# Row sums of a 64 MiB tensor: splitting the rows 112 and 16 per partition instead of 120 and 8

## The chip, the cores and the metric

The kernel runs on one core of one Trainium2 chip. The metric is device time in microseconds (us), span of the program plus what the launch adds; lower is better.

## The reference

```python
batch, seq, dim = 32, 512, 1024
x = np.random.randn(batch, seq, dim).astype(np.float32)     # 16384 rows of 4 KiB, 67.1 MB
divisor = float(dim)

def reference(x, divisor):
    return (np.sum(x, axis=-1) / divisor).astype(np.float32)   # 16384 numbers
```

Every byte of `x` has to come from HBM once, and almost nothing goes back (64 KiB).

## The kernel before

Each of the 128 partitions gets 128 rows. They are cut in two parts: a main part of `M` = 120 rows per partition, contiguous in HBM for each partition, and a last part of `L` = 8 rows per partition. The main part's sums are stored while the last part is still on its way; the sums of the last part leave in a small store at the very end. Pieces get smaller towards the end, so that little work is left when the last bytes arrive. VectorE sums most rows; ScalarE takes some of the late ones (`on_act`), through an activation that also accumulates.

```python
    L = 8
    M = J - L                                      # J = 128
    x_main = bass.AP(tensor=x.tensor, offset=0, ap=[[M * D, P], [D, M], [1, D]])
    x_last = bass.AP(tensor=x.tensor, offset=P * M * D, ap=[[L * D, P], [D, L], [1, D]])
    o_main = bass.AP(tensor=out.tensor, offset=0, ap=[[M, P], [1, M]])
    o_last = bass.AP(tensor=out.tensor, offset=P * M, ap=[[L, P], [1, L]])

    main = [(2, 0)] + [(14, 0)] * 6 + [(14, 4), (12, 5), (8, 4)]     # (rows, of them on ScalarE)
    last = [(4, 2), (2, 1)]
    bulk = ctx.enter_context(tc.tile_pool(name="bulk", bufs=3))
    one = ctx.enter_context(tc.tile_pool(name="one", bufs=1))
    # ... PSUM pool for the activations' unused output
    res = one.tile([P, M], F32, name="res")        # sums of the main part
    fin = one.tile([P, L], F32, name="fin")        # finished sums of the last part
    q = one.tile([P, L], F32, name="q")
    r = one.tile([P, L], F32, name="r")
    nc.gpsimd.memset(r, 0.0)

    j = 0
    for rows, on_act in main:
        t = bulk.tile([P, 14, D], F32, name="t")
        load(t[:, :rows, :], x_main[:, j : j + rows, :])
        sums(res[:, j : j + rows], t, rows, on_act)
        j += rows
    j = 0
    for rows, on_act in last:
        t = one.tile([P, rows, D], F32, name=f"t{rows}")
        load(t, x_last[:, j : j + rows, :])
        sums(q[:, j : j + rows], t, rows, on_act)
        j += rows
    # ... then one whole row (tile row), and the last row in three parts (pa, pb, pc), all loaded from x_last
    nc.gpsimd.tensor_scalar_mul(out=res, in0=res, scalar1=scale)
    tc.keep_in_program_order(nc.sync.dma_start(out=o_main, in_=res))      # the large store
    # ... sums of the last row's parts; fin = q * scale + r; the last column of fin
    tc.keep_in_program_order(nc.sync.dma_start(out=o_last, in_=fin))      # the last store
```

## Time and profile before

| | before |
|---|---|
| median of runs | 161.48 us (three runs, 161.44 to 161.75; with a fourth run: 161.50) |
| span in the profile | 159.9 us |
| VectorE busy | 121.1 us (76%) |
| ScalarE busy | 19.7 us (12%) |
| read from HBM | 67.11 MB, 420 GB/s over the span |

How to read it: no compute engine is busy throughout (VectorE, the busiest, has 76% of the span), and the DMA row of the page is at 9 tenths or more in 32 of the 40 slices. The lines themselves are in the prediction below.

Two more things can be taken from the trace that no view prints. It has a record of each DMA packet (one run of bytes of one partition, with its start and duration; a 14-row load is 128 packets of 57344 B, eight on each of the 16 DMA engines), and the time at which each of the 16 engines reports its share of a load as landed.

### The profile page before, as it was taken

The page shows a single profiled execution, that of the slowest core. Times are in us where ns is not written, and L with a number is a line of the kernel's source. Part 1 is how long each engine was busy: PE and PEld are TensorE (multiplying, and loading weights), DVE is VectorE, ACT ScalarE, POOL GpSimd, SP SyncE. Part 2 cuts the span into 40 slices and gives each one's busy share as a digit, 9 for nine tenths or more (in the row PEclk, how much of TensorE's full clock was granted, in tenths as well). Part 3 has the DMA queues.
Part 4 walks back from the last instruction along what each step waited for, and adds up shares of the span by engine and source line. Part 5 has one row for each costly group of instructions (what it writes and reads, how often), then busy time and mean ns, then how long its engine had stood idle before and what let it go on. Part 6 is the DMA issues. An engine that isn't in the chain of part 4 may idle for free.

```text
span 159.9 us, 139 instructions
## 1 busy us (share of the span) xinstructions
DVE 121.1 (76%) x17; ACT 19.7 (12%) x37; POOL 0.8 (1%) x6
## 2 busy tenths in 40 slices
DVE  0500059995999599968999699959995995494985
ACT  3000000000000000000000000000001900480973
POOL 0000000000000000000000000000000000000010
DMA  7999999987999999987999999987999999999993
GB/s 271 451 459 459 459 459 459 459 373 330 445 459 459 459 459 459 459 387 316 445 459 459 459 459 459 459 387 330 430 459 426 393 578 406 393 393 393 418 408 109
DMA packets 2592, 67.18 MB, mean 420 GB/s; under 512 B 544, under 2 KB 928, under 8 KB 1056
## 3 DMA queue, kind: packets, MB, share of 16 engines
q1 hardware_dynamic: 2592, 67.18, 97.9%
HBM read 67.11 MB, written 0.07 MB: 420 GB/s over the span
## 4 chain that ended last, share of the span: by engine, by line
DMA 77%; DVE 22%; SPq 1%; issue 0%; DVEq 0%
DMA t<-in_x_dram 56%; DMA row<-in_x_dram 21%; DVE res L153 20%; SPq L142 1%; DVE q L173 1%; DVE scaled L195 0%; DVE pc L190 0%; DVE fin L191 0%; DVEq L195 0%; DVEq L229 0%
## 5 line engine op out<-in xcount | busy, mean ns | idle before, releaser
L153 DVE TENSOR_REDUCE res<-t 128x14 f32<-128x14336 f32 (+4 forms) x10 | 115.7, 11566 | 36.4 <-DMA t<-in_x_dram 36.4
L147 ACT ACTIVATE junk<-t 128x1024 f32<-128x1024 f32 x16 | 16.2, 1014 | 136.0 <-DMA t<-in_x_dram 136.0
L153 DVE TENSOR_REDUCE q<-t 128x2 f32<-128x2048 f32 (+1 forms) x2 | 3.5, 1753 | 0.7 <-DMA t<-in_x_dram 0.7
L147 ACT ACTIVATION_READ_ACCUMULATOR junk<-t 128x1 f32 x16 | 3.0, 189 | 0.0
L147 ACT ACT_TABLE_LOAD x1 | 1.3, 1283 | 1.7 <-PEq L215 1.7
L186 POOL TENSOR_SCALAR res<-res 128x120 f32<-128x120 f32 x1 | 0.5, 513 | 150.3 <-DVE res L153 150.3
L173 DVE TENSOR_REDUCE q<-row 128x1 f32<-128x768 f32 x1 | 1.0, 953 | 0.1
L195 DVE TENSOR_SCALAR_CACHE_REDUCE scaled<-pc 128x322 f32<-128x322 f32 x1 | 0.5, 490 | 0.1
L147 ACT ACTIVATE junk<-pa 128x448 f32<-128x448 f32 x1 | 0.5, 548 | 0.1
L190 DVE TENSOR_REDUCE pc<-pb 128x1 f32<-128x256 f32 x1 | 0.4, 411 | 0.0
L147 ACT ACTIVATE junk<-row 128x256 f32<-128x256 f32 x1 | 0.4, 388 | 0.1
L191 DVE SCALAR_TENSOR_TENSOR fin<-q,r 128x7 f32<-128x7 f32 x1 | 0.2, 166 | 0.0
L147 ACT ACTIVATION_READ_ACCUMULATOR junk<-row 128x1 f32 x1 | 0.2, 187 | 0.0
L147 ACT ACTIVATION_READ_ACCUMULATOR junk<-pa 128x1 f32 x1 | 0.2, 187 | 0.0
L139 POOL MEMSET r<- 128x8 f32 x1 | 0.1, 105 | 1.3 <-POOLq L215 1.3
L215 POOL MEMSET const-bfloat16-1.0<- 128x1 bf16 x1 | 0.1, 103 | 0.0
L215 POOL MEMSET const-uint8-127<- 128x1 uint8 x1 | 0.1, 102 | 0.0
L215 POOL MEMSET const-float32-0.0<- 128x1 f32 x1 | 0.1, 99 | 0.2 <-issue 0.2
L215 POOL MEMSET const-float32-1.0<- 128x1 f32 x1 | 0.1, 99 | 0.0
L195 DVE DVE_READ_ACCUMULATOR scaled<-pc 128x1 f32 x1 | 0.1, 83 | 0.0
## 6 DMA issues: line engine op xcount, KB each, us to landing
t<-in_x_dram SPq DMA_DIRECT2D x7, 7168.0 KB, 35.7
t<-in_x_dram SPq DMA_DIRECT2D x1, 6144.0 KB, 33.3
t<-in_x_dram SPq DMA_DIRECT2D x1, 4096.0 KB, 26.0
t<-in_x_dram SPq DMA_DIRECT2D x2, 1024.0 KB, 18.7
t<-in_x_dram SPq DMA_DIRECT2D x1, 2048.0 KB, 30.6
row<-in_x_dram SPq DMA_DIRECT2D x1, 512.0 KB, 33.4
pa<-in_x_dram SPq DMA_DIRECT2D x1, 224.0 KB, 33.5
pc<-in_x_dram SPq DMA_DIRECT2D x1, 160.0 KB, 33.2
```

The costliest lines, as they stand in the source:

```text
L139: nc.gpsimd.memset(r, 0.0)
L142: tc.keep_in_program_order(nc.sync.dma_start(out=dst, in_=src))
L147: nc.scalar.activation(junk[:, :n], src, COPY, scale=by, accum_out=dst)
L153: nc.vector.reduce_sum(out=dst[:, :d], in_=t[:, :d, :], axis=AX)
L173: nc.vector.reduce_sum(out=q[:, j : j + 1], in_=row[:, :c], axis=AX)
L186: nc.gpsimd.tensor_scalar_mul(out=res, in0=res, scalar1=scale)
L190: nc.vector.reduce_sum(out=pc[:, D - b + 1 :], in_=pb, axis=AX)
L191: nc.vector.scalar_tensor_tensor(out=fin[:, : L - 1], in0=q[:, : L - 1], scalar=scale, in1=r[:, : L - 1], op0=MULT, op1=ADD)
L195: nc.vector.tensor_scalar(out=scaled, in0=pc, scalar1=scale, scalar2=0.0, op0=MULT, op1=ADD, accum_out=fin[:, L - 1 :])
L215: nc = _bacc.Bacc("TRN2", target_bir_lowering=False, num_devices=1)
```

## The change

The 8-row piece moves from the main part to the last part: 112 + 16 rows. Intent: the main result is complete one piece earlier, so that the large store is issued earlier; and the last store writes 64 B per partition instead of 32.

```diff
-    L = 8
+    L = 16
     M = J - L
@@
-    main = [(2, 0)] + [(14, 0)] * 6 + [(14, 4), (12, 5), (8, 4)]
-    last = [(4, 2), (2, 1)]
+    main = [(2, 0)] + [(14, 0)] * 6 + [(14, 4), (12, 5)]
+    last = [(8, 4), (4, 2), (2, 1)]
@@
     for rows, on_act in last:
-        t = one.tile([P, rows, D], F32, name=f"t{rows}")
+        if rows == 8:
+            t = bulk.tile([P, 14, D], F32, name="t")[:, :8, :]
+        else:
+            t = one.tile([P, rows, D], F32, name=f"t{rows}")
         load(t, x_last[:, j : j + rows, :])
```

## The prediction

> **What bounds the kernel now.** I read the page first (busy shares, DMA row, chain), then the timeline of the last third, then the chain in order of time, then the DMA issues. The page's chain:
>
> ```profile
> DVE 121.1 (76%) x17; ACT 19.7 (12%) x37; POOL 0.8 (1%) x6
> DMA packets 2592, 67.18 MB, mean 420 GB/s; under 512 B 544, under 2 KB 928, under 8 KB 1056
> DMA 77%; DVE 22%; SPq 1%; issue 0%; DVEq 0%
> ```
>
> No compute engine is full; DMA has 77% of the chain. That DVE has 22% is only how the chain is followed: it passes through reduces because a later load waits for a buffer. The timeline tells whether DVE truly delays the loads:
>
> ```profile
> 55.65 15.09 DVE L153 TENSOR_REDUCE res<-t 128x14 f32<-128x14336 f32 x1 [1.86 <-DMA t<-in_x_dram]
> 72.59 15.09 DVE L153 TENSOR_REDUCE res<-t 128x14 f32<-128x14336 f32 x1 [1.86 <-DMA t<-in_x_dram]
> 89.53 15.09 DVE L153 TENSOR_REDUCE res<-t 128x14 f32<-128x14336 f32 x1 [1.85 <-DMA t<-in_x_dram]
> ...
> 137.94 7.62 DVE L153 TENSOR_REDUCE res<-t 128x7 f32<-128x7168 f32 x1 [3.72 <-DMA t<-in_x_dram]
> ...
> 147.66 4.42 DVE L153 TENSOR_REDUCE res<-t 128x4 f32<-128x4096 f32 x1 [2.09 <-DMA t<-in_x_dram]
> ```
>
> It does not. Each 14-row reduce starts 16.94 us after the one before and lasts 15.09 us; the 1.85 us between is waiting for data. A 14-row load is 7.34 MB (7168 KB on the page), so the stream delivers 7.34 MB / 16.94 us = 433 GB/s. The later pieces come equally fast: the 8-row piece lands 147.66 - 137.94 = 9.72 us after the 12-row one, 4.19 MB / 9.72 us = 432 GB/s. So the load stream is one unbroken transfer, and only the start before it and the tail after it could change. The tail, from the chain in order of time:
>
> ```profile
> 122.95 33.36 DMA row<-in_x_dram
> 156.31 0.02 issue
> 156.34 0.96 DVE q L173
> 157.30 0.02 issue
> 157.32 0.17 DVE fin L191
> 157.49 0.34 DVE pc L190
> 157.83 0.04 DVEq L195
> 157.86 0.07 issue
> 157.93 0.49 DVE scaled L195
> 158.42 0.01 DVEq L229
> ```
>
> From the arrival of the last whole row (156.31) VectorE works serially until 158.42; the last store is issued at 158.46 and the span ends at 159.9. The two stores:
>
> ```profile
> out_dram<-res SPq DMA_DIRECT2D x1, 60.0 KB, 5.2
> out_dram<-fin SPq DMA_DIRECT2D x1, 4.0 KB, 1.4
> ```
>
> The 60 KB store is issued at 152.70 (timeline) and lands 5.2 us later, about 157.9. The 4 KB store takes 1.4 us from issue to landing and ends the span. Before issuing it, the sync engine waits for the landing of everything else, the 60 KB store included: that wait is met 0.55 us before VectorE's result is (158.44), so the 60 KB store is close to the end, but not on the path.
>
> [...]
> - [...]
> - [...] The stores' elements go from 480 to 448 B and from 32 to 64 B[...] (mean 8.5 ns for 32 B, 26.9 ns for 480 B in its packet records)[...].
> - [...] the 60 KB store, issued at 152.70, lands 0.2 us after the last load (issued 124.45, 33.2 us to landing, 157.65). It waited its turn behind loads issued 28 us earlier.
> - [...] Here the pitch goes from 480 to 448 KiB in the main part and from 32 to 64 KiB in the last part[...]. The trace before shows no pitch effect: the packet records of 57344 B (480 KiB pitch, 2118 ns) and 4096 B (32 KiB pitch, 161.9 ns) give (2118 - 161.9) / 53248 B = 0.03674 ns per byte and 11.4 ns fixed; that predicts 613 ns for the 16384 B packets of the 4-row load (32 KiB pitch, measured 614) and 1215 for the 32768 B ones (480 KiB pitch, measured 1215). One line fits both pitches.
>
> **The change part by part.** The order of instructions on each engine is the same, by count and kind, with the same waits; sizes and targets differ.
> 1. **Loads.** The same fifteen-odd transfers of the same sizes in the same order; only HBM addresses differ. By the line above a packet's time depends on its size alone: 0.
> 2. **The 8-row piece** (4-row reduce 4.42 us on VectorE, 4 rows x (1.01 + 0.19 overlapping) us on ScalarE) writes to the small tile instead of the main result. Same durations, same place: 0.
> 3. **The main result is complete one piece earlier.** GpSimd's scaling (0.51 us) waits for the reduce that now ends at 137.94 + 7.62 = 145.56 rather than 152.1; the store is issued near 146.1 + 0.05 rather than 152.70. But all loads have been issued by 124.9, so it still stands behind them in each ring, and lands right after the last one: about 157.87 instead of 157.88, its 8 packets per engine being 32 B smaller (32 x (26.9 - 8.5) / 448 = 1.3 ns each, 0.01 us in all). It has 0.55 us of slack, so 6.5 us of earlier issue buys 0 at the end.
> 4. **The combining operation on VectorE** (fin<-q,r) goes from 7 to 15 elements. VectorE's slope is (15086 - 2287) ns / 12288 elements = 1.04 ns per element, so +8 ns, on the serial tail.
> 5. **The last store** goes from 32 to 64 B per partition, 8 packets per engine. In the packet records it is issued at 158.46, its packets run from 159.30 to 159.49, and it lands at 159.87: 0.84 us to start, 0.19 us moving, 0.38 us confirming. Only the middle part depends on size: +1.3 ns x 8 = +0.01 us.
> 6. GpSimd's first fill, 16 instead of 8 columns, at 1.75 us: hidden, 0.
>
> Sum: 0.008 + 0.01 = +0.02 us, so 161.48 + 0.02 = **161.5 us**.
>
> **The rivals.**
> - **Wider elements make the last store quicker.** [...] 64 B ones might save part of the 0.38 us. I would not give it more than 0.2: 161.3 us. For it: this seems the intent. Against: 1.4 us is mostly fixed[...].
> - **The earlier store gets between the loads.** If the rings let it pass, its 8 packets x 26 ns = 0.2 us per engine come ahead of the last row, which shifts the tail: 161.7 us. Against: the 5.2 us wait in the ring seen before.
> - **The new pitch slows the last 16 rows.** They take 157.65 - 137.94 = 19.7 us. [...] Against: one line for two pitches, one of them the power of two 32 KiB[...]. For: this pitch is untried here.
> - **The 60 KB store was the true gate of the end.** Then freeing it would gain up to 0.5 us: 161.0 us. Against: it lands at 157.9, VectorE ends at 158.4, and it stays behind the loads anyway.
>
> **Range and chances.** The three runs before spread 161.44 to 161.75, 0.31 us, more than any effect that I sum. I add the two small rivals on either side (-0.2 and +0.2) to the scatter: 161.1 to 161.9 us. [...]
>
> **What would show each step.** In the changed profile: 14-row reduces still 16.94 us apart (step 1); the 8-row piece still landing about 9.7 us after the 12-row one and the last row at 156.3 (pitch; later means that rival); GpSimd's scaling near 145.6 and the store's time to landing grown from 5.2 to about 11.7 us (step 3; about 2 us to landing instead means that it passed the loads); the combining operation near 174 ns (step 4); the last store still at 1.4 us (step 5; 1.2 or less speaks for wide elements). The prediction is wrong if the last row's landing moves by more than 0.3 us or the last store by more than 0.2 us.

## The result, and the profile after

| | runs | median | all runs (us) |
|---|---|---|---|
| before | 4 | 161.50 | 161.48, 161.75, 161.44, 161.52 |
| after | 4 | 161.31 | 161.31, 161.27, 161.31, 161.58 |

The ratio is 0.9989, with a 95% interval of 0.9971 to 1.0006: the same within 2%, inside the predicted range of 161.1 to 161.9, and 0.19 us below the predicted 161.5. A ratio is the mean time of one kernel's runs over that of the other's of the same rounds, so not quite the ratio of the medians.

Now the lines after that answer to those of before. First the bulk and the pieces behind it, from the timeline of VectorE, with GpSimd's scaling (columns: start, duration, engine and line, operation, what it writes and reads; in brackets the idle time before it and what ended that):

```profile
106.47 15.09 DVE L153 TENSOR_REDUCE res<-t 128x14 f32<-128x14336 f32 x1 [1.85 <-DMA t<-in_x_dram]
...
145.65 0.49 POOL L189 TENSOR_SCALAR res<-res 128x112 f32<-128x112 f32 x1 [143.80 <-DVE res L153]
...
147.66 4.42 DVE L153 TENSOR_REDUCE q<-t 128x4 f32<-128x4096 f32 x1 [2.09 <-DMA t<-in_x_dram]
```

The 8-row piece is reduced at 147.66 exactly as before, and into `q` now; GpSimd scales at 145.65 instead of 152.16. Then the tail, from the chain in order of time:

```profile
122.91 33.25 DMA row<-in_x_dram
156.16 0.02 issue
156.18 0.96 DVE q L176
157.14 0.03 issue
157.17 0.18 DVE fin L194
157.34 0.34 DVE pc L193
157.68 0.04 DVEq L198
157.72 0.07 issue
157.79 0.49 DVE scaled L198
```

The tail is the same work, but it starts when the last whole row lands, at 156.16 instead of 156.31. From there to the last store's issue it takes 2.15 us in both (158.31 - 156.16; 158.46 - 156.31). Last, the two stores in the DMA view (size, and time from issue to landing):

```profile
out_dram<-res SPq DMA_DIRECT2D x1, 56.0 KB, 11.5
out_dram<-fin SPq DMA_DIRECT2D x1, 8.0 KB, 1.4
```

The large store waits 11.5 us instead of 5.2, and the wide last store takes 1.4 us as the narrow one did (1.42 against 1.41 in the trace). So neither of the intended effects reaches the end. Yet the last six loads took less time: from the landing of the 8-row piece (147.63 in both) to that of the last load 9.87 us instead of 10.04. I had expected nothing there, and the question for the experiments was whether that is real, and what makes it.

### The profile page after: what moved, and what is told of

It is laid out like the page before. It is cut to its first block, busy times and chain, and to the rows that moved or that the text cites. A ratio compares the mean times of both kernels' runs of the same rounds, so it can differ in the third digit from the quotient of the medians.

```text
span 159.8 us, 139 instructions
## 1 busy us (share of the span) xinstructions
DVE 121.1 (76%) x17; ACT 19.6 (12%) x37; POOL 0.8 (0%) x6
## 4 chain that ended last, share of the span: by engine, by line
DMA 76%; DVE 22%; SPq 1%; issue 0%; DVEq 0%
DMA t<-in_x_dram 56%; DMA row<-in_x_dram 21%; DVE res L153 20%; SPq L142 1%; DVE q L176 1%; DVE scaled L198 0%; DVE pc L193 0%; DVE fin L194 0%; DVEq L198 0%; DVEq L232 0%
## 5 line engine op out<-in xcount | busy, mean ns | idle before, releaser
L153 DVE TENSOR_REDUCE res<-t 128x14 f32<-128x14336 f32 (+3 forms) x9 | 111.2, 12360 | 34.3 <-DMA t<-in_x_dram 34.3
L153 DVE TENSOR_REDUCE q<-t 128x4 f32<-128x4096 f32 (+2 forms) x3 | 7.9, 2642 | 2.7 <-DMA t<-in_x_dram 2.5
L189 POOL TENSOR_SCALAR res<-res 128x112 f32<-128x112 f32 x1 | 0.5, 494 | 143.8 <-DVE res L153 143.8
```

Of the source, the lines that this page charges most:

```text
L153: nc.vector.reduce_sum(out=dst[:, :d], in_=t[:, :d, :], axis=AX)
```

## The experiments

The first four compare three theories. NOISE: nothing but scatter. ADDRESS: the new HBM addresses make the last loads quicker. STORE: the earlier store does. The first eleven runs were made on one chip; the kernel before had 161.38 us there in nine runs (161.26 to 161.45).

**1. The changed kernel once more.** No edit.

> The changed kernel once more, to learn whether its 0.19 us are real. Three theories. NOISE: the two kernels differ by nothing but scatter; ratio within 0.9990 to 1.0010, and in the trace the last whole row lands anywhere between 156.15 and 156.35. ADDRESS: the last loads read HBM at a pitch of 64 instead of 32 KiB and arrive a little sooner; ratio about 0.9988, and from the landing of the 8-row piece (147.63) to that of the last load about 9.87 us instead of 10.04. STORE: the large store, issued at 152.7 in the kernel before, disturbs the last loads, and issued at 146.2 it does so no more; same ratio of 0.9988. The prediction's rival that the wide last store gains is already at odds with the trace (1.42 against 1.41 us).

Measured: 161.34 us (161.26 to 161.37), ratio 0.9998 (0.9984 to 1.0011). The kernels are equal on this chip. But the last six loads were again quicker: 9.83 us. So the stage is not noise, although the whole time is hardly different: something else must have become slower.

**2. The large store held back.** In the changed kernel:

```diff
-    res = one.tile([P, M], F32, name="res")
+    res = one.tile([P, M + 8], F32, name="res")
@@
+    nc.gpsimd.tensor_scalar_mul(out=res[:, M:], in0=q[:, :8], scalar1=scale)
     nc.gpsimd.tensor_scalar_mul(out=res, in0=res, scalar1=scale)
-    tc.keep_in_program_order(nc.sync.dma_start(out=o_main, in_=res))
+    tc.keep_in_program_order(nc.sync.dma_start(out=o_main, in_=res[:, :M]))
```

> The changed kernel with its large store held back until the 8-row piece is summed, as before: GpSimd first scales the eight sums of that piece. STORE: the store is issued near 152.7 to 153.2 again and the time goes back up to about 161.5, ratio near 1.000 to the kernel before; last loads as slow as before (10.04 us from the 8-row piece to the last load). ADDRESS and NOISE: no change against the changed kernel, 161.3 and 9.87 us for ADDRESS, anything within scatter for NOISE. The prediction's step 3 (slack of 0.55 us) also says no change.

Measured: 161.50 us (161.40 to 161.56), the last six loads 10.07 us. As STORE expects. (Note the first line of the edit: the tile became 32 B wider. I took it for harmless.)

**3. The changed kernel at the old HBM addresses.** Wrong result on purpose.

```diff
-    x_main = bass.AP(tensor=x.tensor, offset=0, ap=[[M * D, P], [D, M], [1, D]])
-    x_last = bass.AP(tensor=x.tensor, offset=P * M * D, ap=[[L * D, P], [D, L], [1, D]])
+    x_main = bass.AP(tensor=x.tensor, offset=0, ap=[[120 * D, P], [D, 120], [1, D]])
+    x_last = bass.AP(tensor=x.tensor, offset=P * 120 * D, ap=[[8 * D, P], [D, 8], [1, D]])
     # and the loads of the last part index them as the kernel before does
```

> The changed kernel, but all loads read the HBM addresses of the kernel before (480 KiB and 32 KiB pitch); same instructions, same store times; wrong result on purpose, since sums go to other places. ADDRESS: back to about 161.5 and 10.04 us from the 8-row piece to the last load. STORE: stays at 161.3 and 9.87 us. NOISE and the prediction's pitch step: no difference from the changed kernel beyond scatter of 0.15 us.

Measured: 161.19 us (161.16 to 161.25), the last six loads 9.76 us. ADDRESS falls: with the old addresses the time does not go back up, it goes further down.

**4. The kernel before at the new HBM addresses.** The reverse edit; wrong result.

> The kernel before, but all loads read the HBM addresses of the changed kernel (448 KiB and 64 KiB pitch); the large store still at 152.7, last store still 32 B; wrong result on purpose. ADDRESS: about 161.3, ratio 0.9988, 9.87 us from the 8-row piece to the last load. STORE: 161.5, ratio 1.000, 10.04 us. NOISE: ratio within 0.9990 to 1.0010.

Measured: 161.53 us (161.47 to 161.59), the last six loads 10.06 us. Three lines of VectorE's timeline in each, the first reduce, that of the 8-row piece and that of the last whole row; first of run 3, then of run 4:

```profile
4.70 2.29 DVE L153 TENSOR_REDUCE res<-t 128x2 f32<-128x2048 f32 x1 [4.70 <-DMA t<-in_x_dram]
...
147.53 4.42 DVE L153 TENSOR_REDUCE q<-t 128x4 f32<-128x4096 f32 x1 [2.09 <-DMA t<-in_x_dram]
...
156.02 0.95 DVE L176 TENSOR_REDUCE q<-row 128x1 f32<-128x768 f32 x1
```

```profile
4.92 2.29 DVE L153 TENSOR_REDUCE res<-t 128x2 f32<-128x2048 f32 x1 [4.92 <-DMA t<-in_x_dram]
...
147.76 4.42 DVE L153 TENSOR_REDUCE res<-t 128x4 f32<-128x4096 f32 x1 [2.09 <-DMA t<-in_x_dram]
...
156.45 0.95 DVE L173 TENSOR_REDUCE q<-row 128x1 f32<-128x768 f32 x1
```

From the second line to the third run 3 takes 8.49 us, run 4 8.69 us, and run 4 is already 0.23 us later at the second, 0.22 of it from the first line on. Four kernels make a square:

| | structure of before | structure of after | difference |
|---|---|---|---|
| old HBM addresses | 161.38 (before) | 161.19 (run 3) | -0.19 |
| new HBM addresses | 161.53 (run 4) | 161.34 (run 1) | -0.19 |
| difference | +0.15 | +0.15 | |

So the change has two effects on the loads that nearly cancel: its new HBM addresses cost 0.15 us, and something in the rest of it saves 0.19 us. The 95% interval of each ratio to the kernel before holds 1 (that of run 4, 0.9999 to 1.0024, only just); but the five runs of 3 and those of 1 and 4 do not overlap, and the two columns agree.

The traces show where the address cost lies. The first reduce, which waits for the first load, starts at 4.66 to 4.83 us (mean 4.74) in the six kernels of this document with the old addresses, and at 4.78 to 4.94 us (mean 4.87) in the seven with the new ones, one trace of each. From there to the reduce of the 8-row piece all take 142.80 to 142.85 us. So about 0.12 us of the 0.15 is there before the first load has landed, and none comes from the bulk of the stream.

What saves the 0.19 us, STORE explained so far. One thing spoke against it: in the packet records the loads were quicker from about 148 us on, 4 us before the store of the kernel before was even issued.

**5. A pitch of 512 KiB.** The kernel before with one block of 128 rows per partition.

```diff
-    ... offset=0, ap=[[M * D, P], [D, M], [1, D]])             # and the outputs likewise
-    ... offset=P * M * D, ap=[[L * D, P], [D, L], [1, D]])
+    ... offset=0, ap=[[J * D, P], [D, M], [1, D]])
+    ... offset=M * D, ap=[[J * D, P], [D, L], [1, D]])
```

> The kernel before with one block of 128 rows per partition: a pitch of 512 KiB in all loads (it was 480 and 32), instructions and times of the stores unchanged; right result. Of the first four runs: the addresses of the changed kernel cost about 0.15 us (161.53 against 161.38), there from the first loads on. If the pitch were a matter of large powers of two (the prediction's rival), 512 KiB in the whole stream would show it sixteen times as strongly: packets of 57344 B well over 2118 ns and a time above 165. If only small shifts of phase are at work, the packets stay at 2118 ns and the time stays within 161.2 to 161.7.

Measured: 161.99 us (161.73 to 162.19), ratio 1.0043 (1.0030 to 1.0055), a loss clear of noise, though small, and neither expectation: 0.6 us, between nothing and 4 us. VectorE's timeline of this run shows where:

```profile
5.08 2.29 DVE L153 TENSOR_REDUCE res<-t 128x2 f32<-128x2048 f32 x1 [5.08 <-DMA t<-in_x_dram]
21.99 15.09 DVE L153 TENSOR_REDUCE res<-t 128x14 f32<-128x14336 f32 x1 [14.62 <-DMA t<-in_x_dram]
38.92 15.09 DVE L153 TENSOR_REDUCE res<-t 128x14 f32<-128x14336 f32 x1 [1.85 <-DMA t<-in_x_dram]
...
138.21 7.62 DVE L153 TENSOR_REDUCE res<-t 128x7 f32<-128x7168 f32 x1 [3.73 <-DMA t<-in_x_dram]
```

The first load is 0.25 us late (5.08 against 4.83), the 14-row loads still come about 16.93 us apart, and at the 12-row piece the lag is 0.27 us (138.21 against 137.94). So in this profiled run (161.73 us, the quickest of the six) most of the loss is a late start, and not a slower stream; a packet of 57344 B takes 2122 ns on the mean against 2118. What the other runs, up to 162.19 us, lost beyond that was not traced.

**6. The large store on ScalarE's queue.** In the changed kernel:

```diff
-    tc.keep_in_program_order(nc.sync.dma_start(out=o_main, in_=res))
+    nc.scalar.dma_start(out=o_main, in_=res)
```

> The changed kernel with its large store issued from ScalarE's queue at about 146.2 instead of the sync engine's. RING (step 3 of the prediction): on a ring of its own the store need not wait behind the loads: it lands about 2 us after issue, near 148.5, instead of 157.7, and takes its 8 packets x 25 ns = 0.2 us from the 4-row load, so the last loads move later by up to 0.2 us, time 161.5. If it still lands at 157.7, the order is not the ring's. EARLY QUEUE (a store that stands queued behind the loads makes them quicker, which the late-store kernel lost): with the store out of the loads' ring their packets are as slow as before (4-row packets 614 instead of 611 ns), time 161.5 or more.

Measured: 161.45 us (161.30 to 161.57). The DMA view:

```profile
out_dram<-res ACTq DMA_DIRECT2D x1, 56.0 KB, 7.7
```

RING holds: issued at 146.18, the store lands at 153.87, before the 2-row load, and no longer behind the loads. It takes 7.7 us where I had expected 2. Its packets move between 149.7 and 153.1, in between the load packets, and the 4-row load takes 0.14 us longer than in run 1 (147.59 to 152.56, 4.97 us, against 4.83). EARLY QUEUE as I had put it falls: packets of the loads were at 611 ns with the store on another ring. (The edit also moved the issue of the last load, `pc`, from 124.4 to 137.89; so it did in run 11. It still landed last of the loads.)

**7. The kernel before with the store split.** 112 columns stored early, 8 at the old time. Right result.

```diff
-    res = one.tile([P, M], F32, name="res")
+    res = one.tile([P, M - 8], F32, name="res")
+    res8 = one.tile([P, 8], F32, name="res_b")      # the sums of the 8-row piece go here
@@
-    tc.keep_in_program_order(nc.sync.dma_start(out=o_main, in_=res))
+    tc.keep_in_program_order(nc.sync.dma_start(out=o_main[:, : M - 8], in_=res))
+    nc.gpsimd.tensor_scalar_mul(out=res8, in0=res8, scalar1=scale)
+    tc.keep_in_program_order(nc.sync.dma_start(out=o_main[:, M - 8 :], in_=res8))
```

> The kernel before with its addresses, but 112 of the 120 columns are stored as soon as they are done (about 146.2) and the 8 of the 8-row piece in a store of their own at about 152.7; right result. EARLY QUEUE: the early issue is what helps, so the last loads are as quick as in the run with early store and old addresses: 9.77 us from the 8-row piece to the last load, 161.2. LATE ISSUE (a store issued at 152.7 disturbs the loads then in flight): the loads are slow from 152.7 on, 161.3 to 161.4.

Measured: 161.41 us (161.39 to 161.52), the last six loads 10.08 us. With 112 of the 120 columns issued for storing at 146.15, the loads are as slow as before. EARLY QUEUE falls again; and LATE ISSUE cannot make packets slow (613.9 ns in the 4-row load) from 148 us on, four microseconds ahead of the store issued at 152.40.

**8. One more transfer queued behind the loads.** The kernel before plus an 8 KB load that nobody uses.

```diff
+    spare = one.tile([P, 16], F32, name="spare")
+    load(spare, x_last[:, 0, :16])
```

> The kernel before with one more load of 64 B per partition queued behind all others at about 138 (8 KB, used by nothing). EARLY QUEUE as a matter of any transfer queued behind the loads: packets of the 4-row load and later at 611, 309, 159, 74 ns and the time near 161.2 in spite of the extra transfer. If only a store does it, or only one issued near 146, the packets stay at 614, 313, 162, 75 ns and the time at 161.4.

Measured: 161.38 us (161.37 to 161.52), the last six loads 10.09 us. No effect.

**9 and 10. Who waits.** By now the quick runs were those in which GpSimd was finished and nothing was left to store by 146 us; run 5 alone was against it. Two kernels part the waits, both from the changed one.

```diff
# 9: GpSimd has one more thing to wait for
+    held = one.tile([P, 8], F32, name="held")
+    nc.gpsimd.tensor_scalar_mul(out=held, in0=q[:, :8], scalar1=scale)
# 10: the sync engine first stores the raw sums of the 8-row piece, then the large result
+    tc.keep_in_program_order(nc.sync.dma_start(out=o_last[:, :8], in_=q[:, :8]))
     tc.keep_in_program_order(nc.sync.dma_start(out=o_main, in_=res))
```

> The changed kernel with one more small operation on GpSimd, of no use, that waits until the 8-row piece is summed (about 152.1); the large store is still issued near 146.2 and nothing is stored at 152. So far, where GpSimd was finished and nothing was left to store by 146, packets of the last loads ran at their minimum from 148 on (4-row packets 611, 2-row 309, last parts 74, 46, 55 ns) and the time was lower by 0.17 us; where a store came at 152 they ran at 614, 313, 75, 46.5, 60. GPSIMD WAITS (a waiting GpSimd is what disturbs): 614 ns, 161.5. SYNC WAITS or STORE AT 152: 611 ns, 161.34.

> The changed kernel, but the sync engine first waits for the eight sums of the 8-row piece and stores them raw (32 B per partition, overwritten by the last store), and only then issues the large store; both near 152.3. GpSimd is finished at 146.2 as in the changed kernel. GPSIMD WAITS: packets of the 4-row load at 611 ns, about 161.34. SYNC WAITS or STORE AT 152: 614 ns, 161.5.

Measured: 161.40 us (161.31 to 161.53) and 161.40 us (161.26 to 161.55), beside 161.42 of the kernel before (161.33 to 161.51, eight runs). These times decide nothing; the packets do. In both they ran at 611, 309, 74, 46 and 55 ns, the quick pattern. In run 10 everything that STORE needs was undone. The DMA view:

```profile
out_dram<-res SPq DMA_DIRECT2D x1, 56.0 KB, 5.2
out_dram<-q SPq DMA_DIRECT2D x1, 4.0 KB, 5.5
```

Both stores were issued at 152.1 and 152.6, as late as before, and still the last six loads took 9.81 us. All three theories of these two runs fall, and with them STORE in every form.

**11. Split store on two queues.** Run 7 with the small store on ScalarE's queue.

> The kernel before with its addresses, 112 columns stored early by the sync engine (near 147.7) and the other 8 from ScalarE's queue near 152.5; right result. It is the candidate for the gain of early store and old addresses together (161.19 in the run with the wrong result). SYNC WAITS: the sync engine has nothing more to issue after 147.7, so packets at their minimum and about 161.2. GPSIMD WAITS or STORE AT 152: as the kernel before, 161.4, or a little more as the small store on a ring of its own comes between the last loads (8 packets of 9 ns).

Measured: 161.56 us (161.30 to 161.62), the last six loads 10.06 us; no gain, and the widest scatter of all but run 5.

**What sorts the runs.** Listed by what differs in SBUF instead of by who waits, they fall apart at once. `res` lost 8 columns (-32 B) and `fin`, `q` and `r` won 8 each (+96 B), so all tiles behind them moved up by 64 B. In the built programs the first of the load tiles, `t4`, starts at byte 189120 of a partition before, 192 past a multiple of 256, and at 189184 after, which is 739 x 256. The sizes of `t4`, `t2`, `row`, `pa` and `pb` are multiples of 256 B, so all six share the remainder.

| run | tiles start past a multiple of 256 B | 4-row packets, ns | 2-row | pa | pb | pc | last six loads, us |
|---|---|---|---|---|---|---|---|
| before | 192 | 614.3 | 313.2 | 75.4 | 46.6 | 60.8 | 10.04 |
| 4 | 192 | 614.8 | 313.4 | 75.2 | 46.5 | 60.4 | 10.06 |
| 7 | 192 | 613.9 | 313.2 | 75.4 | 46.6 | 60.7 | 10.08 |
| 8 | 192 | 614.4 | 313.6 | 75.4 | 46.6 | 60.8 | 10.09 |
| 11 | 192 | 614.5 | 313.3 | 74.5 | 46.0 | 55.1 | 10.06 |
| 2 | 32 | 615.0 | 314.2 | 75.4 | 46.5 | 61.0 | 10.07 |
| 5 | 192 | 612.2 | 311.2 | 74.0 | 46.0 | 55.0 | 10.01 |
| after | 0 | 611.3 | 309.0 | 74.0 | 46.0 | 55.0 | 9.87 |
| 1 | 0 | 611.3 | 309.0 | 74.0 | 46.0 | 55.0 | 9.83 |
| 3 | 0 | 611.3 | 309.0 | 74.0 | 46.0 | 55.0 | 9.76 |
| 6 | 0 | 611.3 | 309.0 | 74.0 | 46.0 | 55.0 | 9.96 |
| 9 | 0 | 611.2 | 309.0 | 74.0 | 46.0 | 55.0 | 10.04 |
| 10 | 0 | 611.3 | 309.0 | 74.0 | 46.0 | 55.0 | 9.81 |

Run 2, the pillar of STORE, was slow because its edit widened `res` by 32 B and pushed the tiles to 32 past. Run 3, with old HBM addresses but the tiles of after, had them at 0; run 4 at 192. The square above is right, but its columns are alignment of tiles, not time of store. A last run takes this by itself.

**12. The kernel before with the tiles aligned.** One line; the rest of the kernel, stores included, as before, and a right result.

```diff
-    r = one.tile([P, L], F32, name="r")
+    r = one.tile([P, L + 16], F32, name="r")
```

> The kernel before with one difference: a small tile is made 64 B wider per partition, so that the tiles of the last six loads start at a multiple of 256 B in SBUF (before: 192 B past one); addresses in HBM, stores and their times as before; right result. ALIGNMENT: in every run so far but the one with 512 KiB pitch, packets of the last loads ran at their minimum exactly where their tiles started at a multiple of 256 B, and above it where they started 192 or 32 B past one; which of the two it was followed from the widths of the result tiles that the change altered. Then here packets of the 4-row load take 611 ns (before 614), 2-row 309 (313), last parts 74, 46, 55 (75, 46.6, 61), from the 8-row piece to the last load about 9.8 us instead of 10.04, and the time falls by 0.15 to 0.2 us, to about 161.2, although the large store is still issued at 152.7. STORE: packets as before, time as before (161.4).

Measured, on another chip: 161.20 us (161.15 to 161.34), beside 161.41 (161.33 to 161.56, nine runs) of the kernel before; ratio 0.9989 (0.9975 to 1.0003). Packets at 611.3, 309.0, 74.0, 46.0 and 55.0 ns, the last six loads 9.76 us. The start and the end of the tail from the chain, and the large store:

```profile
156.04 0.96 DVE q L173
...
157.63 0.49 DVE scaled L195
```

```profile
out_dram<-res SPq DMA_DIRECT2D x1, 60.0 KB, 4.9
```

The large store has its old size and its old time (issued at 152.61), and yet the last row's sum starts at 156.04, 0.30 us before that of the kernel before (156.34). Of this 0.09 us were there before the last six loads began (8-row piece landed at 147.54 instead of 147.63; the first reduce was as much earlier, 4.74 against 4.83, within what the kernels with the old addresses differ by); the rest is the loads' own. The longer packets alone, eight of each load on an engine, make 0.14 us of the 0.28 us between 10.04 and 9.76 (an estimate from the means of `before` and of this run); the rest lies outside the packets' own durations and was not traced. This kernel is the best with a right result, though what it gains on either kernel is within what the interval leaves open; the trace shows the cause, the time alone would not.

What stays open. Run 5 had unaligned tiles, but packets at the minimum for the last row's parts (74.0, 46.0, 55.0 ns) and between the two groups before (612.2, 311.2), and run 11 had its last two loads so (46.0 and 55.1 ns), so an unaligned start does not always cost: in both, other disturbances were in the stream (other HBM addresses; a store on a second ring), and no run tells how these interact. Run 9 had quick packets, but gaps between them (10.04 us), most in the whole row's load, whose packets of 4096 B took 172.8 ns instead of 159. That load's packets show the same in `after` and in run 1 (172.1 and 174.1), and 159.0 in runs 3 and 12 with the old addresses. But runs 10 and 6, which have the new addresses and aligned tiles too, show 160.4 and 159.7: they alone of these five issue the large store late or on another ring. Run 3 issues it early and has the old addresses. So in these traces it takes both, and no run was made to test that. Why the new addresses delay the first load is not shown either.

Nor do the runs tell whether a multiple of 256 B is needed: no small tile started 128 past one, and 189184 is a multiple of 128 as well. The tiles of the large loads start 128 past in every kernel here. A line through the aligned packets of 16384 and 4096 B (611.3 and 159.0 ns) puts their 57344 B packets at 2119 ns, an estimate, and they took 2118.0: no cost of that start can be seen. Aligning them was not tried.

## Why the prediction was right or wrong

The time was predicted rightly, as the same within a small range, and so were five of the six parts. In part that was luck: the sixth had missed two effects of opposite sign, and the room below 161.5 in the range came from a rival (wide elements) that proved wrong.

- **What bounds the kernel.** Right. In every run the 14-row reduces start 16.94 us apart or within 0.02 of it, whatever was done to stores and addresses. That is 433 GB/s; whether the bulk of the stream could go faster no run shows.
- **Step 2, the 8-row piece.** Right: 4.42 us at 147.66 in both.
- **Step 3, the earlier store buys nothing.** Right, and its working too: issued at 146.17 (predicted 146.15), 11.5 us to landing (11.7), still behind the last load (157.71 after 157.50). Its rival, a store among the loads, was seen in run 6, with the store on another ring (7.7 us to landing); it cost about what was predicted for the rival (0.14 us in the 4-row load, 0.2 predicted).
- **Step 4, the combining operation.** Right: 176 ns after, 166 before, +8 predicted.
- **Step 5, the last store.** Right: 1.42 against 1.41 us, +0.01 predicted. Its packets of 64 B took 10.5 ns on the mean against 8.5 for 32 B; the start took 0.84 us in both, the moving 0.21 against 0.19 us, and the time from the last packet's end to landing 0.37 against 0.38 us. The rival of wide elements falls.
- **Step 6.** Right: the fill grew by 7 ns (112 instead of 105) at 1.75 us, hidden.
- **Step 1, "By the line above a packet's time depends on its size alone: 0".** This step failed, though at a size that the range held. In these traces a packet's time also went with where it starts in SBUF (16384 B: 614.3 ns at 192 past, 611.3 aligned), and the start of the first reduce, which waits for the first load, with where the loads read (4.74 and 4.87 us on the mean). The change moves both: 64 B in SBUF saved 0.19 us, the new HBM addresses cost 0.15 us. Together that is the -0.04 us of the chip of the experiments (161.34 against 161.38), and not the -0.19 us of the result. The result's interval holds both values; in its two traces the first reduce starts at 4.83 alike, so in them the saving stands alone. My line was fitted through packets of 57344 and 4096 B to four digits, and I read its agreement (613 against 614 ns) as proof, when 3 ns per packet were just what was at stake. I had also read "sizes and targets differ" from the instructions and looked at HBM targets only. Nor was the whole stream at one rate, as I took it from the 12- and 8-row pieces: the last six loads carry as many bytes as the 8-row piece and took 10.04 us to its 9.72. That was the room; aligned they took 9.76.
- **The rival of the pitch.** No trace had shown a size for it. It had the sign of the 0.15 us, but the last 16 rows did not slow: with 64 KiB instead of 32 they took 19.56 us (157.50 - 137.94) against 19.7. Even 512 KiB in the whole stream costs 0.6 us, and the profiled run, 0.3 us slower in span than the kernel before, has 0.25 us of it before the first load has landed.

## What to carry to other kernels

Here a change in the widths of small tiles moved all tiles behind them in SBUF by 64 B (`t4` from byte 189120 to 189184), and the 4-row packets went from 614.3 to 611.3 ns. So print the addresses before giving a small difference to the change's intent, and before trusting an experiment that adds a column. Here a store issued on the queue that carries the loads waited behind them (11.5 us to landing), so issuing it earlier gained nothing while its landing had slack (0.55 us before); on a second queue it passed (7.7 us) and the 4-row load took 0.14 us longer. When the time is the same, look at whether two effects cancel: two edits crossed in a square showed it here, while the two kernels' medians alone showed nothing.
